# A two-layer decoder trunk with routed experts: one-hot rows written a chunk ahead, small experts two chunks behind the large ones

## The chip, the cores and the metric

The kernel runs on one core of one Trainium2 chip, in one launch. The time is the device time of the program in microseconds (us), smaller is better. Engines are named as in the profile: PE is TensorE (PEld its weight load), DVE VectorE, ACT ScalarE, POOL GpSimd, and SP the engine whose queue issues the DMAs here. The span runs from the first to the last instruction.

## The reference

A sequence of 256 tokens of width 1024 in float32 goes through two layers. Layer 0 has an attention and a state-space half and then a dense SwiGLU block; layer 1 has two kinds of attention and then a routed block of eight SwiGLU experts. The change lies in that last block alone:

```
logits = t @ router                       # t: 256 tokens x 1024, after an RMS norm
top_val, top_idx = top_k(logits, 2)       # two of eight experts for each token
top_w = softmax(top_val)
gates = sum(one_hot(top_idx, 8) * top_w)
for e in range(8):                        # each expert has 1024 -> 2816 -> 1024
    out += gates[:, e] * ((silu(t @ w_gate[e]) * (t @ w_up[e])) @ w_down[e])
return x + out
```

The weights of one expert are 3 x 1024 x 2816 floats. All eight experts are read from memory once, which is 264 pieces ("units") of 1 MB.

## The kernel before, in words

Up to the routing, a recorder (lines 71 to 317) takes down the operations and writes them out in an order of its own. From the first expert on the recorder is off (line 1629), and every engine gets its instructions in the order in which the code is written.

The eight experts are sorted by how many tokens chose them. The first four (BIG = 4) are "large": they get 128 rows each, and each product is made of three matmuls on split operands (a high part wh and a low part wl, lines 522 to 524). The last four are "small": 64 rows each, in plain float32, two of them side by side on PE.

An expert is worked in 11 chunks (FC) of 256 hidden columns. A chunk has three units of weights: gu0 and gu1 (gate and up columns, for the two halves of the input width) and dn (the down rows). The list `steps` (lines 1594 to 1605) sets the order: chunk g of the large experts runs beside chunk g - LAG of the small ones, LAG being 4. So the first LAG chunks belong to large experts alone, and the last ones to small experts alone.

Before an expert can start, its rows must be picked from the 256 normalised tokens (xnh and xnl are their high and low part). That is a matmul with a one-hot matrix: `one_hots` writes the matrix on DVE by comparing positions (poso) with a row of counters, and `gather_all` makes one of the eight 128-row products and lets ACT write it out. Both are called in the step "rest", which follows gu1 of a large chunk (lines 1672 to 1689): the small experts' products (into xs) in the first chunks of the first large expert (p = 0), those of large experts 1 and 2 (into xl) from chunk LAG + 2 of p = 0 on, and those of large expert 3 from chunk 2 of p = 1 on.

```
def one_hots(lo, n, width=P):
    t = tw(2 * n * width, dt=F32R).rearrange("p (b e s) -> p b e s", b=2, e=n)
    for b in range(2):
        V.tensor_tensor(t[:, b], ..., ..., OP.is_equal)     # DVE
def gather_all(k, oh, dst):
    o, gain = gather(k, ..., n * w)                         # four matmuls on PE
    S.activation(dst[:, :, k], ..., AF.Copy, scale=gain)    # ACT
```

Ahead of "rest", the step gu1 does the elementwise part of the chunk and calls `st.ahead(HL)` twice (lines 1653 to 1655): each call splits one coming unit of a large expert into wh (two ACT instructions) and wl (two DVE instructions), until three units stand ready. A third call follows after the transposes ("tr"). The tile `tw` is one of a set of 12 working tiles.

The units come in the order in which the steps use them, through the class `Stream`. It has twelve places to load into: five tiles "raw", and xres, xg0, xg1 (both "xg" in the profile), more, fl, wx and wy. xg0 is given up once 14 units have been asked for (XG = 14), because xl is put there. A large unit's place is free once it is split, a small unit's once PE has read it. Loads are issued on SP in one queue, in order. The units of the first large expert lie at a fixed address; all others need the expert's number from the routing (`ids`, read into a register by SP at line 1615). While the recorder is on, `load` stops at the first unit whose address needs that number (lines 718 and 719).

Of the kernel before, what the change touches and what calls it, by code (L numbers as in the profile page):

```python
# [19 lines left out]
P = 128  # L20
# [32 lines left out]
XG = 14  # L53
BIG = 4
HALFP = 64
LAG = 4
PAIRED = 0.65
WARM = 10
FIRST = 9
# [335 lines left out]
def kernel(ctx: ExitStack, tc: tile.TileContext, a, out: bass.AP):  # L395
# [29 lines left out]
    def tw(n=512, np_=P, dt=F32):  # L425
        return rec.tile(wkp, [P, 512], dt, "tw", TW, name="tw")[:np_, :n]

    def pa():
        return rec.tile(psp, [P, 512], F32, "ps", 8, name="ps")
# [104 lines left out]
    def bc(ap, shape):  # L534
        return ap.to_broadcast(shape)
# [237 lines left out]
    def ff_gu(st, xs, gu, u, ahead=True):  # L773
        wh, wl = st.next(ahead)
        for b in range(len(xs)):
            for kk in range(4):
                k = 4 * u + kk
                mm3(gu[b], xs[b][0][:, k, :], xs[b][1][:, k, :], wh[:, kk * 512:(kk + 1) * 512],
                    wl[:, kk * 512:(kk + 1) * 512], k == 0, k == 7)

    def ff_act(gu, scales=None, act=None):
        hs = []
        for b in range(len(gu)):
            si = tw(256)
            hh = tw(256)
            if scales:
                tact(si, gu[b][:, 0:256], AF.Silu, scale=scales[b])
                V.scalar_tensor_tensor(hh, gu[b][:, 256:512], scales[b], si, op0=OP.mult, op1=OP.mult)
            else:
                (act or tact)(si, gu[b][:, 0:256], AF.Silu)  # L790
                V.tensor_tensor(hh, gu[b][:, 256:512], si, OP.mult)
            hs.append(hh)
        return hs

    def ff_tr(hs):
        n = 2 * len(hs) * P
        tp = pa()
        transposes([h[:, i * P:(i + 1) * P] for i in range(2) for h in hs], tp)
        th, tl = tw(n, dt=F32R), tw(n, dt=F32R)
        S.activation(th, tp[:, :n], AF.Copy)  # L800
        V.tensor_tensor(tl, tp[:, :n], th.bitcast(F32), OP.subtract)
        return th, tl
# [73 lines left out]
    for g in range(2):  # L876
# [13 lines left out]
        for c in range(4):  # L890
            j = 4 * g + c
# [188 lines left out]
    mo = scope("m")  # L1080
# [389 lines left out]
# [4 lines that stand above are left out]
            V.tensor_tensor(t[:, b], bc(iota[:, None, 0:width], [P, n, width]),  # L1474
                            bc(poso[:, b, lo:lo + n, None], [P, n, width]), OP.is_equal)
        return t

    def both_halves(r):

        t = tw(256, dt=F32R).rearrange("p (b s) -> p b s", b=2)  # L1480
        for b in range(2):
            V.tensor_scalar(t[:, b].rearrange("p (i s) -> p i s", i=2), bc(iota[:, None, 0:HALFP], [P, 2, HALFP]),
                            poso[:, b, r:r + 1], None, op0=OP.is_equal)
        return t
# [6 lines left out]
    def gather(k, ohs, n):  # L1491

        o = pa()[:, 0:n]
        for i, src in enumerate((xnh, xnl)):
            for b in range(2):
                mmx(o, src[:, b, k * P:(k + 1) * P], ohs(b), i + b == 0, i + b == 2)
        return o, k2("gf1k", k, k + 1)
# [5 lines left out]
    def gather_all(k, oh, dst):  # L1503

        n, w = oh.shape[2], oh.shape[3]
        o, gain = gather(k, lambda b: oh[:, b].rearrange("p e s -> p (e s)"), n * w)
        S.activation(dst[:, :, k], o.rearrange("p (e s) -> p e s", e=n), AF.Copy, scale=gain)
# [17 lines left out]
    def scatter(t, y, g, acc, store=False):  # L1525
        for i in range(2):
            rec.late = HALF if i else 0
            cs = slice(i * 512, (i + 1) * 512)
            for b in range(2):
                sp = pa()  # L1530
                T.matmul(sp, t[:, b * P:(b + 1) * P], y[i][0], start=True, stop=False)
                T.matmul(sp, t[:, b * P:(b + 1) * P], y[i][1], start=False, stop=True)
                V.scalar_tensor_tensor(acc[:, b, cs], sp, g(b), acc[:, b, cs], op0=OP.mult, op1=OP.add)
                if store:
                    dma(ov[:, b, cs], acc[:, b, cs])
        rec.late = 0
# [5 lines left out]
    def large_split(src):  # L1542
        x = large_tile()
        S.activation(x[0], src, AF.Copy)
        V.tensor_tensor(x[1], src, x[0].bitcast(F32), OP.subtract)
        return x


    def sm_gu(xs, gu, u):
        w = st.next(False)  # L1550
        for kk in range(4):
            k = 4 * u + kk
            wv = w[:, kk * 512:(kk + 1) * 512].rearrange("p (g f) -> p g f", g=2)
            for i in range(2):
                mmx(gu[i * HALFP:(i + 1) * HALFP, 0:256].rearrange("p (g f) -> p g f", g=2), xs[:, k],
                    wv[:, :, i * P:(i + 1) * P], k == 0, k == 7)
        st.done()

    def sm_act(gu):
        si, hh = tw(P), tw(P)  # L1560
        tact(si, gu[:, 0:P], AF.Silu)
        V.tensor_tensor(hh, gu[:, P:256], si, OP.mult)
        return hh

    def sm_tr(hh):
        tp = pa()
        transposes([hh], tp)
        t = tw(P)
        S.activation(t, tp[:, 0:P], AF.Copy)
        return t  # L1570

    def sm_dn(t, y, first, last):
        w = st.next(False)
        for hf in range(2):
            for i in range(2):
                mmx(y[hf][i * HALFP:(i + 1) * HALFP, :], t[:, i * HALFP:(i + 1) * HALFP],
                    w[:, i * 1024 + hf * 512:i * 1024 + (hf + 1) * 512], first, last)
        st.done()
# [12 lines left out]
    def chunk(sm, g):  # L1591
        return (sm, *divmod(g, FC)) if 0 <= g < BIG * FC else None

    steps = []
    for g in range(BIG * FC + LAG + 1):
        l, l0, s, s0 = chunk(False, g), chunk(False, g - 1), chunk(True, g - LAG), chunk(True, g - LAG - 1)
        if l and s0:
# [38 lines left out]
    for n, (k, it) in enumerate(steps):  # L1636
        if k == "late":
            while pend:
                scatter(*pend.pop(0))
            continue  # L1640
        sm, p, c = it
        if k in ("gu0", "gu1"):
            if k == "gu0":
                gu[sm] = pa()
            if sm:
                sm_gu(xs[:, p], gu[sm], unit_of[k])
            else:
                ff_gu(st, [xb], [gu[sm]], unit_of[k], False)
            if k == "gu1":
                hs[sm] = sm_act(gu[sm]) if sm else ff_act([gu[sm]])  # L1650
                if not sm and c == FC - 1 and p < BIG - 1:
                    xb = large_split(xl[:, p % 2])
                if not sm:
                    st.ahead(HL)
                    st.ahead(HL)
                if c == 0:
                    ohs[sm] = n, both_halves(BIG + p) if sm else one_hots(p, 1)[:, :, 0]
        elif k == "tr":
            ts[sm] = sm_tr(hs[sm]) if sm else ff_tr(hs[sm])
            if not sm:  # L1660
                st.ahead(HL)
        elif k == "dn":
            if c == 0:
                ys[sm] = [pa(), pa()]
            if sm:
                sm_dn(ts[sm], ys[sm], c == 0, c == FC - 1)
            else:
                ff_dn(st, ts[sm], [ys[sm]], c == 0, c == FC - 1, False)
            if c == FC - 1:
                r = p + (BIG if sm else 0)  # L1670
                pend.append((ohts[sm], y_split(ys[sm]), lambda b, r=r: gateo[:, b, r:r + 1], x3, n == len(steps) - 2))
        else:
            for e in list(ohs):
                if n >= ohs[e][0] + 5:
                    o = ohs.pop(e)[1]
                    ohts[e] = oht_of(o[:, 0], o[:, 1])
            if p == 0 and c < LAG:
                for j in range(2 * c, 2 * c + 2):
                    gather_all(j, oh_s, xs)
            if p == 0 and LAG + 2 <= c < LAG + 6:  # L1680
                if c == LAG + 2:
                    xl, oh_l = mo([P, 2, 8, P], "xg0"), one_hots(1, 2)
                for j in range(2 * (c - LAG - 2), 2 * (c - LAG - 1)):
                    gather_all(j, oh_l, xl)
            if p == 1 and 2 <= c < 6:
                if c == 2:
                    oh_l = one_hots(3, 1)
                for j in range(2 * c - 4, 2 * c - 2):
                    gather_all(j, oh_l, xl[:, 0:1])
    man.close()  # L1690
# [179 lines left out]
```

## Time and profile before

| | us |
|---|---|
| median of 3 runs (1150.53 to 1153.55) | 1151.38 |
| the profiled execution | 1152.82 |
| its span | 1151.0 |
| PE busy | 1113.1 (97%) |
| DVE busy | 723.1 (63%) |
| ACT busy | 601.4 (52%) |
| DMA queue, share of 16 engines' span | 76.0% |

The expert stage starts near 469 us and takes the rest of the span. A PE that is shown as busy is not at its peak, as matmuls overlap: what counts is where the next one starts. Two other things are to be read beside it, the granted clock (1.00 is 2.4 GHz, 0.50 is 1.2 GHz) and the rate at which the DMA queue moves bytes. The first queue that runs without a gap is a limit of its own, whatever PE does.

### The profile page before, as it was taken

The numbers are of one execution on the slowest core, as the hardware profiler recorded it, in microseconds if no ns is written. First come the engines' busy times: TensorE is split into PE (matmuls) and PEld (weight loads), VectorE is DVE, ScalarE is ACT, GpSimd is POOL, SyncE is SP. The second block draws the span as 40 slices with busy tenths as digits, with TensorE's granted clock in tenths as the row PEclk, the third lists the DMA queues.
The fourth block names the chain that finished last, engine by engine and source line by source line (L and its number), as shares of the span: only waits on it lengthen the run. The fifth ranks groups of instructions, "written<-read, shape, count | busy, mean of one in ns | idle before, by whom it ended". The sixth has DMA issues, their size and how long they took to land.

```text
span 1151.0 us, 16659 instructions
## 1 busy us (share of the span) xinstructions
PE 1113.1 (97%) x6100; PEld 833.5 (72%) x6100; DVE 723.1 (63%) x1325; ACT 601.4 (52%) x1134; POOL 29.1 (3%) x59
## 2 busy tenths in 40 slices
PE   8999999999999999998999799999999999999997
PEld 7887888888787877875676567666666666676653
DVE  6999954544388867785356646556556556565542
ACT  5868644444378656474355435545454554544430
POOL 1050000000300000000000000000000000000000
PEclk9999999999999999899899999999999999999999
DMA  9551555556343633379799989999999999999996
GB/s 345 214 215 37 185 218 188 186 181 218 113 156 124 254 149 147 144 272 382 289 401 408 411 333 390 414 422 422 421 421 420 423 421 422 421 422 422 421 422 248
DMA packets 52216, 348.15 MB, mean 302 GB/s; under 512 B 5920, under 2 KB 6048, under 8 KB 11680
## 3 DMA queue, kind: packets, MB, share of 16 engines
q1 hardware_dynamic: 52128, 347.02, 76.0%
q8 instruction: 50, 0.82, 0.3%
q14 instruction: 38, 0.31, 0.1%
HBM read 345.95 MB, written 1.05 MB: 301 GB/s over the span
## 4 chain that ended last, share of the span: by engine, by line
PE 89%; DMA 5%; DVE 3%; ACT 2%; issue 0%; SPq 0%; DVEq 0%; ACTq 0%
PE ps L333 23%; PE ps L522 19%; PE ps L524 19%; PE ps L523 19%; PE ps L328 10%; DMA raw<-in_moe_dram 3%; DMA more<-in_moe_dram 2%; DVE wl L333 1%; ACT tw L328 1%; DMA raw<-in_w_dram 0%; DVE wl L328 0%; DVE tw L328 0%; ACT wh L333 0%; DVE xres L333 0%; ACT wh L328 0%
## 5 line engine op out<-in xcount | busy, mean ns | idle before, releaser
L333 ACT ACTIVATE tw<-ps 128x256 fp32r<-128x256 f32 (+3 forms) x202 | 72.6, 365 | 360.8 <-PE ps L524 212.5
L522 PE MATMUL ps<-wh,fh 128*128 128x512 f32 (+2 forms) x632 | 254.5, 403 | 0.0
L523 PE MATMUL ps<-wl,fh 128*128 128x512 f32 (+2 forms) x632 | 245.5, 389 | 0.0
L333 DVE TENSOR_TENSOR tw<-ps,tw 128x256 f32<-128x256 f32 (+3 forms) x158 | 64.6, 427 | 264.7 <-ACT tw L333 264.7
L333 DVE TENSOR_TENSOR wl<-raw,wh 128x1024 fp32r<-128x1024 f32 x156 | 183.7, 1224 | 55.9 <-ACT wh L333 55.4
L333 ACT ACTIVATE wh<-raw 128x1024 fp32r<-128x1024 f32 x156 | 155.2, 1050 | 43.7 <-PE ps L524 37.8
L524 PE MATMUL ps<-wh,fh 128*128 128x512 f32 x352 | 138.5, 394 | 0.0
L522 PEld LDWEIGHTS ps<-wh,fh 128*128 128x128 f32 x632 | 119.4, 189 | 22.2 <-issue 0.2
L523 PEld LDWEIGHTS ps<-wl,fh 128*128 128x128 f32 x632 | 119.4, 189 | 21.7 <-issue 0.2
L524 PE MATMUL ps<-wh,fl 128*128 128x512 f32 (+2 forms) x280 | 107.6, 384 | 0.0
L522 PE MATMUL ps<-wh,tw 128*128 128x512 f32 (+1 forms) x252 | 103.2, 410 | 1.8 <-ACT tw L333 1.1
L524 PE MATMUL ps<-wh,tw 128*128 128x512 f32 (+1 forms) x252 | 99.3, 394 | 0.0
L523 PE MATMUL ps<-wl,tw 128*128 128x512 f32 (+1 forms) x252 | 99.2, 394 | 0.0
L333 PE MATMUL ps<-raw,xs 128*64 128x256 f32 x672 | 78.4, 379 | 0.0
L524 PEld LDWEIGHTS ps<-wh,fh 128*128 128x128 f32 x352 | 66.4, 189 | 14.5
L328 DVE TENSOR_TENSOR wl<-raw,wh 128x512 fp32r<-128x512 f32 x113 | 74.7, 680 | 2.9 <-ACT wh L328 2.9
L333 PEld LDWEIGHTS ps<-raw,xs 128*64 128x64 f32 x672 | 47.9, 137 | 33.4 <-issue 11.7
L328 ACT ACTIVATE wh<-raw 128x512 fp32r<-128x512 f32 (+1 forms) x104 | 59.7, 620 | 18.7 <-PE ps L524 11.5
L524 PEld LDWEIGHTS ps<-wh,fl 128*128 128x128 f32 x280 | 52.6, 188 | 10.7 <-DVE fl L328 0.2
L522 PEld LDWEIGHTS ps<-wh,tw 128*128 128x128 f32 x252 | 47.6, 189 | 15.0 <-ACT tw L333 2.2
L524 PEld LDWEIGHTS ps<-wh,tw 128*128 128x128 f32 x252 | 47.4, 188 | 11.4 <-DVE tw L328 0.4
L523 PEld LDWEIGHTS ps<-wl,tw 128*128 128x128 f32 x252 | 47.5, 189 | 9.3
(319 smaller groups left out, 1744.2 us busy)
## 6 DMA issues: line engine op xcount, KB each, us to landing
raw<-in_moe_dram SPq DMA_DIRECT2D x120, 1024.0 KB, 13.9
raw<-in_ffn_dram SPq DMA_DIRECT2D x30, 1024.0 KB, 4.8
xg<-in_moe_dram SPq DMA_DIRECT2D x24, 1024.0 KB, 13.4
more<-in_moe_dram SPq DMA_DIRECT2D x24, 1024.0 KB, 12.9
fl<-in_moe_dram SPq DMA_DIRECT2D x24, 1024.0 KB, 13.2
raw<-in_w_dram SPq DMA_DIRECT2D x23, 1024.0 KB, 4.9
wx<-in_moe_dram SPq DMA_DIRECT2D x23, 1024.0 KB, 14.2
xres<-in_moe_dram SPq DMA_DIRECT2D x23, 1024.0 KB, 14.0
```

Of the source, the lines that this page charges most:

```text
L328: return (self.name, self.cost(fn, args, kw), lambda: real(*args, **kw))
L333: return getattr(self.eng, fn)(*args, **kw)
L522: nc.tensor.matmul(ps, xh, wh, start=start, stop=False)
L523: nc.tensor.matmul(ps, xh, wl, start=False, stop=False)
L524: nc.tensor.matmul(ps, xl, wh, start=False, stop=stop)
```

## The change

Three things are done. LAG goes from 4 to 2: the small experts run two chunks behind the large ones. The eight products for the small experts are made four a chunk in two chunks, not two a chunk in four. And the one-hot matrices of large experts 1 and 2, and of large expert 3, are written in the "rest" of the chunk before the one whose "rest" has their first product (chunk 3 of p = 0, with products from chunk 4 on; chunk 1 of p = 1, with products from chunk 2 on). Products for large experts 1 and 2 also start two chunks earlier, since they are placed by LAG.

```
-LAG = 4
+LAG = 2
...
             if p == 0 and c < LAG:
-                for j in range(2 * c, 2 * c + 2):
+                for j in range(8 // LAG * c, 8 // LAG * (c + 1)):
                     gather_all(j, oh_s, xs)
+            if (p, c) in ((0, LAG + 1), (1, 1)):
+                oh_l = one_hots(1, 2) if p == 0 else one_hots(3, 1)
             if p == 0 and LAG + 2 <= c < LAG + 6:
                 if c == LAG + 2:
-                    xl, oh_l = mo([P, 2, 8, P], "xg0"), one_hots(1, 2)
+                    xl = mo([P, 2, 8, P], "xg0")
                 for j in range(2 * (c - LAG - 2), 2 * (c - LAG - 1)):
                     gather_all(j, oh_l, xl)
             if p == 1 and 2 <= c < 6:
-                if c == 2:
-                    oh_l = one_hots(3, 1)
                 for j in range(2 * c - 4, 2 * c - 2):
                     gather_all(j, oh_l, xl[:, 0:1])
```

How instructions move is shown at three places. The first is DVE, in the first large expert, where the one-hot matrix of large experts 1 and 2 is written (`tw<-c_2935,poso 128x256`; `wl<-..` rows are splits, `tw<-ps,tw` the elementwise part of a chunk, CAST the copy of a transposed one-hot). Before:

```order
L333 CAST tw<-ps 128x256
L333 TENSOR_TENSOR tw<-ps,tw 128x128
L333 TENSOR_TENSOR tw<-ps,tw 128x256
L333 TENSOR_TENSOR wl<-wy,wh 128x1024 x2
L333 TENSOR_TENSOR tw<-ps,tw 128x256
L333 TENSOR_TENSOR wl<-raw,wh 128x1024 x4
L333 TENSOR_TENSOR tw<-c_2935,poso 128x256 x2
L333 TENSOR_TENSOR tw<-ps,tw 128x128
```

And with the change:

```order
L333 TENSOR_TENSOR tw<-ps,tw 128x256
L333 TENSOR_TENSOR wl<-raw,wh 128x1024 x2
L333 TENSOR_TENSOR wl<-xres,wh 128x1024 x2
L333 CAST tw<-ps 128x256
L333 TENSOR_TENSOR tw<-c_2935,poso 128x256 x2
L333 TENSOR_TENSOR tw<-ps,tw 128x128
L333 TENSOR_TENSOR tw<-ps,tw 128x256
L333 TENSOR_TENSOR wl<-raw,wh 128x1024 x2
L333 TENSOR_TENSOR tw<-ps,tw 128x256
L333 TENSOR_TENSOR wl<-xg_5203,wh 128x1024 x2
```

The two rows stand behind four rows of splits in both, but with the change the products that read them come one chunk later on PE.

The second place is SP's queue at the end of the recorded part: the loads up to the one that reads the expert's number (L1615), the difference of the two.

```order
 L447 DMA xg_3415<-in_moe_dram 128x2048
 L447 DMA raw<-in_moe_dram 128x2048 x4
-L447 DMA wx<-in_moe_dram 128x2048
 L447 DMA xres<-in_moe_dram 128x2048
-L447 DMA wy<-in_moe_dram 128x2048
-L447 DMA raw<-in_moe_dram 128x2048
-L447 DMA xg_3422<-in_moe_dram 128x2048
-L447 DMA more<-in_moe_dram 128x2048
-L447 DMA fl<-in_moe_dram 128x2048
 L447 DMA raw<-in_moe_dram 128x2048
 L1615 TENSOR_LOAD ids
```

With the one raw load ahead of this piece, 14 units are loaded before the number is known in the kernel before, and 8 with the change, because the ninth unit is now one of a small expert. Behind L1615 the changed queue goes on:

```order
L1615 ISA x2
L443 ISA
L443 DMA raw<-in_moe_dram 128x2048
L443 ISA
L443 DMA xg_4964<-in_moe_dram 128x2048
L443 DMA more<-in_moe_dram 128x2048
L443 DMA fl<-in_moe_dram 128x2048
L443 DMA wx<-in_moe_dram 128x2048
L443 ISA
L443 DMA wy<-in_moe_dram 128x2048
L443 ISA
L443 DMA raw<-in_moe_dram 128x2048
```

Six of the moved loads stand here, as the first of the loads with a run-time address.

The third place is ACT at the first chunks, where the small experts' products are written out (xs); the difference of the two.

```order
 L333 ACTIVATE wh<-raw 128x1024 x4
-L333 ACTIVATE xs<-ps,c_2935 128x4x64 x2
+L333 ACTIVATE xs<-ps,c_2935 128x4x64 x4
 L333 ACTIVATE tw<-ps 128x256
 L333 ACTIVATE wh<-xres 128x1024 x2
 L333 ACTIVATE tw<-ps 128x256
 L333 ACTIVATE wh<-xg_3415 128x1024 x2
```

The first chunk has two more of these instructions behind its four split rows, and the second chunk likewise; the third and fourth have none. PE has 4090 rows in both kernels.

## Rows read from the trace of the kernel before

**Rows 1.** The page: PE's line, and the issue line of the expert loads.

```profile
PE 1113.1 (97%) x6100; PEld 833.5 (72%) x6100; DVE 723.1 (63%) x1325; ACT 601.4 (52%) x1134; POOL 29.1 (3%) x59
raw<-in_moe_dram SPq DMA_DIRECT2D x120, 1024.0 KB, 13.9
```

**Rows 2.** Two long windows: length, engines' busy time, granted clock, DMA share, GB/s.

```profile
467.70:725.00 257.30, 244.05 (x1319) 177.76 (x1319) 149.78 (x193) 127.78 (x193) 0.00 (x0) 0.96 0.88 347
725.00:1136.00 411.00, 407.69 (x2313) 277.27 (x2313) 235.75 (x286) 195.08 (x284) 0.00 (x0) 1.00 1.01 420
```

**Rows 3.** Whom PE waited for from 460 us on: total, times, longest.

```profile
PE ps L333 <- DVE tw L333: 15.6, 6, 6.5
```

**Rows 4.** The timeline around 541 us: start, length, engine, idle before.

```profile
542.50 4.63 DVE L333 TENSOR_TENSOR wl<-raw,wh 128x1024 fp32r<-128x1024 f32 x4 [0.52 <-ACT wh L333]
...
547.05 0.75 DVE L333 TENSOR_TENSOR tw<-c,poso 128x256 fp32r<-128x256 f32 x2
...
547.62 0.82 PE L333 MATMUL ps<-tw,xnh 128*128 128x256 f32 x2 [6.51 <-DVE tw L333]
...
548.90 0.47 ACT L333 ACTIVATE xg<-ps,c 128x256 f32<-128x256 f32 x1 [3.60 <-PE ps L333]
```

**Rows 5.** The timeline at 662 us.

```profile
662.40 0.66 PE L333 MATMUL ps<-tw,xnh 128*128 128x128 f32 x2 [6.37 <-DVE tw L333]
```

**Rows 6.** A short window of PE behind the first wait: length, PE, clock, DMA share, GB/s.

```profile
547.60:550.00 2.40, 2.38 (x10) 0.50 0.93 341
```

**Rows 7.** The chain of waits in order of time: start, length, engine, tile, line.

```profile
526.79 5.91 PE ps L333 x44
...
565.89 6.63 PE ps L333 x50
580.94 6.63 PE ps L333 x50
...
641.71 5.91 PE ps L333 x44
...
679.51 6.53 PE ps L333 x50
694.44 6.53 PE ps L333 x50
...
813.41 5.91 PE ps L333 x44
827.72 5.69 PE ps L333 x42
841.82 5.69 PE ps L333 x42
```

**Rows 8.** PE's timeline of the first chunk ends (a product, chunk 1, chunk 1's product).

```profile
476.04 0.40 PE L333 MATMUL ps<-tw,xnh 128*128 128x256 f32 x2
...
476.99 0.40 PE L522 MATMUL ps<-wh,fh 128*128 128x512 f32 x1
...
485.68 0.48 PE L333 MATMUL ps<-tw,xnh 128*128 128x256 f32 x2
```

**Rows 9.** Windows of 15 us, columns as in rows 2.

```profile
470.00:485.00 15.00, 15.00 (x67) 12.28 (x67) 9.98 (x21) 8.76 (x13) 0.00 (x0) 0.94 0.38 148
...
560.00:575.00 15.00, 15.00 (x89) 10.75 (x87) 8.08 (x10) 7.73 (x12) 0.00 (x0) 1.00 0.65 253
```

**Rows 10.** SP's queue: the first loads with a run-time address.

```profile
467.67 14.93 SPq L443 DMA_DIRECT2D raw<-in_moe_dram  x3
```

**Rows 11.** The end of the chain of waits.

```profile
1089.34 19.81 DMA more<-in_moe_dram
...
1116.07 22.81 PE ps L333 x156
...
1139.23 1.99 PE ps L333 x8
```

**Rows 12.** The last window with loads in it, columns as in rows 2.

```profile
1138.00:1140.00 2.00, 1.63 (x9) 0.48 (x7) 0.00 (x0) 0.28 (x1) 0.00 (x0) 1.00 0.23 88
```

## The prediction, made before the changed kernel was run

> **What bounds the kernel now.** The page comes first: PE is busy for 97% of the span, and every expert load is 1024 KB [rows 1]. That share hides stages with different limits, so the windows of the expert stage come next. Until 725 us the DMA queue is short of work (347 GB/s), from there on it runs at 420 GB/s with a busy share of 1.01 [rows 2]. So two things could set the end: PE, which does the same work whenever it comes, and a queue that is full in the last 411 us but has idle time in the first 257. The list of waits says what PE stands still for: DVE, six times, 15.6 us in all, 6.5 at the longest [rows 3]. The timeline shows the two large ones. At 547.62 PE starts the first product for large experts 1 and 2 after 6.51 us idle; on DVE the one-hot matrix was written at 547.05, straight behind four splits of 4.63 us [rows 4]. At 662.40 the same happens for large expert 3, 6.37 us [rows 5]. Behind such a wait the granted clock is 0.50, that is 1.2 GHz [rows 6]. At the very end the chain runs through a load, 19.81 us from 1089 on, and then 22.81 us of small experts' products on PE [rows 11].
>
> **The one-hots, part by part.** What a wait costs is read from the pace of the chunks, which takes the slow clock in. The chain has one row a chunk [rows 7]. A chunk after a x44 row takes 827.72 - 813.41 = 14.31 us, a plain one 841.82 - 827.72 = 14.10, one with two products of large experts 1 and 2 takes 580.94 - 565.89 = 15.05, one with two of expert 3 takes 694.44 - 679.51 = 14.93. Without the first wait, 526.79 + 14.31 + 15.05 would bring PE to 556.15; the row stands at 565.89. That is 9.74 us: 6.51 idle and 3.2 of slow clock. Without the second, 641.71 + 14.31 + 14.93 = 670.95, and the row stands at 679.51: 8.56 us, of which 6.37 is idle. Together 18.3 us.
>
> The change writes both matrices one chunk earlier, over 14 us before their first reader. The two DVE instructions still cost 0.75 us and 0.48 or so, but in a window like 560 to 575 DVE is busy for 8.08 of 15 us [rows 9], and nothing on PE asks for them in that chunk. If that cover were gone, the price would be these 0.75 us. What is late next at these places is nothing that the trace shows: the tokens' parts xnh and xnl have lain ready since the first products. I take the whole 18.3 us as gone.
>
> **Four products a chunk.** PE makes two products in 476.99 - 476.04 = 0.95 us [rows 8]; eight products cost 3.8 us in two chunks as in four. On ACT a product's output takes 0.47 us [rows 4]. Two more of them in each of the first two chunks, 0.94 us, stand ahead of the copy of the transposes that the down product needs, while ACT is busy for 8.76 of 15 us there [rows 9]. Bounds: nothing, if that copy is still ready when PE has made the products and gu1, and 0.94 us twice if it is late by all of it. PE itself comes 0.95 us later at this point because it makes the two products too, so I take nothing.
>
> **LAG 2 on PE.** PE has as many instructions as before. Two chunks of small experts' work move from the end, where small experts run alone, to the front. At full clock they cost the same there, so the sum is nothing.
>
> **LAG 2 on the DMA queue.** This is the part with a cost that can go either way. A unit is 1.0486 MB, which at 420 GB/s [rows 2] is 2.50 us. Before, 250 units are loaded from 467.67 on [rows 10], now 256, since the ninth unit is already a small expert's and waits for the expert's number. If the queue never pauses, the 256 units take 639 us and the last lands at 1107. Before, 250 units take 624 us, but the last ends near 1138.4 (in the window from 1138 the queue moves 88 GB/s for two us, 0.4 us of work [rows 12]): 46.4 us were gaps, nearly all ahead of 725 (467.7 to 725 at 347 instead of 420 GB/s is 45 us of them).
>
> How many gaps remain? There are 12 places and 3 split units. At 467.67 eight units have been asked for and three are split, so seven places are free, and the queue has 7 x 2.50 = 17.5 us of work at once, where before one free place was followed by a stop: its first three loads went out over 14.93 us [rows 10]. By then PE has moved on. Chunk 0 ends at 476.04, four products take 1.90, chunk 1 takes 485.68 - 476.99 = 8.69 [rows 8], again 1.90 and 8.69: at 497.2 PE has used eight units, and the queue can have brought 8 + 29.5 / 2.50 = 19.8, against room for 14 + 8 = 22. The room is not reached, though places come free in lumps after splits; I allow 4 us of gaps, with 0 and 10 as ends. From then on a pair of chunks uses six units in 14.10 to 15.05 us and the queue brings 5.6 to 6.0, so places stay free. The last load then lands at about 1111.
>
> PE's last down product ended at 1139.23 + 1.99 = 1141.2 [rows 11]; 18.3 us less is 1122.9. The queue is ahead of that by 12 us where it was ahead by 2.8 before. Six small units instead of twelve follow the last unit that must be split, which asks for a lead a little larger; 12 us leaves room. So PE decides and the gain stays. Of the waits behind late loads at the end, which are the 15.6 - 6.51 - 6.37 = 2.7 us left in rows 3, all may go, or 3 more may come, as the queue's lead is drawn down by plain chunks just as before; I take 1 us less.
>
> **The sum.** 18.3 + 1.0 = 19.3 us. The profiled execution took 1152.82 us for a span of 1151.0, so one like it would take 1133.5; the median of the runs is 1.44 below that execution, which gives 1132.1. With the ends named above (2.7 less, or 3 more and 1.9 for the outputs) the gain lies between 13.4 and 21.0 us, 1130 to 1138.
>
> **Rivals.**
>
> *The queue takes part of it back.* Gaps stay because SP issues in order: one load whose place is not free holds up all behind it, as in the 14.93 us of rows 10. If half of the old gaps stay, 23 us, the last load lands at 1130; with the 2.8 us from there to PE's end, some 2 for the shorter tail, and 9.8 from PE's end to the span's, the span is 1144.6, the time 1145. For it: the queue is full for all of the last 411 us [rows 2]. Against: seven places are free at once, and the early chunks use units faster than before. From 13 us of gaps on it costs something, from 31 on nothing is left of the gain.
>
> A page bears on this: the Trainium skill, "DMA: Bandwidth & Descriptors", section "Where 436 GB/s comes from", says that loads from HBM are bound by the HBM side at some 358 GB/s for a core. By that rule 256 units would take 750 us and no change of PE's order could gain. This trace does not bear it out: 420 GB/s over 411 us in rows 2, so the measurement decides, and that rule gets no chance of its own.
>
> *The missing early loads decide.* This is the case on the other side. Six loads that used to land before the expert's number was known come after it, 15 us of queue time. If the gaps behind 467.67 all stay (46.4 us), the last load lands at 1153, and by the same steps the time is 1168. It decides once more than 31 us of gaps stay. For it: 250 and 256 units at the measured rate. Against: the gaps came from full places, and 467.67 is now a time at which seven are empty.
>
> *A wait comes back elsewhere.* xl is written two chunks earlier and lies in the place xg0, and with four products at once more PSUM tiles and more of the twelve working tiles are held. If one such thing stops PE for as long as one of the old waits did, 9 us are lost again: 1142. Nothing in the rows speaks for it except that two waits of this kind did arise.
>
> *It does nothing that can be measured.* Under 0.3% (3.5 us, about what a measurement here can tell from no change), if the queue keeps some 30 us of gaps.
>
> **How the numbers follow.** The forecast 0.70 (0.08 of it below 1130, by waits at the end or a better front than counted), the queue taking part back 0.13, a wait elsewhere 0.09, nothing 0.04, the missing early loads 0.04. The range of eight in ten is 1125 to 1142: it leaves out most of the queue's case and the last two. Faster 0.92, within 0.3% 0.04, slower 0.04.
>
> **What would show it.** In the new profile no idle of 6 us before a product on PE, and a granted clock of 1.00 from about 480 us on; the one-hot rows on DVE one chunk ahead of the first product; the first seven loads behind 467 us within 2 us on SP's queue; the rate above 400 GB/s from 470 us on instead of 347; the row after the first products one chunk's pace behind the one before. The prediction is wrong if PE waits more than 5 us for loads in the last 100 us, if the queue stands still between 485 and 600 us for more than 13 us in all, or if a new wait of some us stands at the first chunks.

## The result, and the profile after

| | before | with the change |
|---|---|---|
| median of 4 runs each | 1152.05 (1150.53 to 1153.55) | 1136.47 (1135.60 to 1137.66) |
| ratio, 95% interval | | 0.9865 (0.9850 to 0.9879) |
| the profiled execution and its span | 1152.82, 1151.0 | 1137.01, 1135.2 |

The change saves 15.6 us (13.9 to 17.3 by the interval). The forecast was 19.3: the sign and the cause are right, some 3.7 us of it did not arrive.

The page of the changed kernel, PE's line, beside [rows 1]:

```profile
PE 1108.8 (98%) x6100; PEld 830.9 (73%) x6100; DVE 723.4 (64%) x1325; ACT 601.3 (53%) x1134; POOL 29.1 (3%) x59
```

PE, with the same 6100 instructions, is busy for 4.3 us less. That is about the slow clock that is gone behind the two waits (3.2 and 8.56 - 6.37 = 2.2 us) less the 1.3 us of it that came at the end (below). The list of waits from 460 us on has this in place of [rows 3] (total, times, longest):

```profile
PE ps L333 <- DVE tw L333: 4.3, 5, 2.7
```

The two long waits are gone from it. The two long windows answer to [rows 2], with the same columns (length, engines' busy time, granted clock, DMA share, GB/s):

```profile
467.70:725.00 257.30, 256.93 (x1447) 185.06 (x1447) 154.99 (x200) 133.31 (x204) 0.00 (x0) 0.99 0.99 406
725.00:1121.00 396.00, 390.89 (x2186) 267.31 (x2184) 227.42 (x275) 189.22 (x274) 0.00 (x0) 1.00 1.00 416
```

In the first, PE no longer stands still (256.93 of 257.30 us, 244.05 before), and the queue moves 406 instead of 347 GB/s. In the second PE is idle for 5.1 of 396 us, before for 3.3 of 411. So the loss must be sought there.

The chain of waits gives the place. Its rows of 44 matmuls stand at the same chunk of large experts 1 to 3 in both kernels (start, length, engine, tile, line). With the change:

```profile
642.61 5.91 PE ps L333 x44
...
805.76 5.91 PE ps L333 x44
...
965.98 5.91 PE ps L333 x44
...
1111.94 11.35 PE ps L333 x74
1123.70 1.99 PE ps L333 x8
```

Before, beside 641.71 and 813.41 in [rows 7] and 1139.23 in [rows 11], the third one:

```profile
973.20 5.91 PE ps L333 x44
```

With the change PE has done two chunks of a small expert more at each of the first three rows. What those are worth is seen at the end: 22.81 us of matmuls before [rows 11] against 11.35 now, 11.46 us. So the changed kernel is ahead by 641.71 + 11.46 - 642.61 = 10.6 us after the first one-hots, by 813.41 + 11.46 - 805.76 = 19.1 after both, by 973.20 + 11.46 - 965.98 = 18.7 at the third row, and by 1139.23 - 1123.70 = 15.5 at the last product. Of each figure 0.44 us were there already at the first product for the small experts (475.60 against 476.04 in [rows 8]). So what was forecast for the one-hots, 18.3 us, had arrived (18.2 at the third row); 3.2 us of it are lost again after 966.

The timeline of PE there (start, length, engine, operation, idle before and who ended it):

```profile
1100.70 1.90 PE L333 MATMUL ps<-wx,xs 128*64 128x256 f32 x16
...
1102.89 1.95 PE L333 MATMUL ps<-more,xs 128*64 128x256 f32 x16
1107.51 0.48 PE L333 MATMUL ps<-cp,tw 128*128 128x128 f32 x1 [2.67 <-DVE tw L333]
...
1108.21 0.63 PE L523 MATMUL ps<-wl,tw 128*128 128x512 f32 x1
1108.64 0.63 PE L524 MATMUL ps<-wh,tw 128*128 128x512 f32 x1
...
1111.87 1.94 PE L333 MATMUL ps<-wy,tw 128*64 128x512 f32 x8
```

And ACT and DVE in the same stretch:

```profile
1103.80 2.00 ACT L333 ACTIVATE wh<-raw 128x1024 fp32r<-128x1024 f32 x2 [6.11 <-DMA raw<-in_moe_dram]
1105.71 0.53 ACT L333 ACTIVATE tw<-ps 128x128 f32<-128x128 f32 x2
...
1104.89 2.36 DVE L333 TENSOR_TENSOR wl<-raw,wh 128x1024 fp32r<-128x1024 f32 x2 [6.74 <-ACT wh L333]
1107.17 0.62 DVE L333 TENSOR_TENSOR tw<-ps,tw 128x128 f32<-128x128 f32 x2
```

Read it backwards. PE stands at the transposes of a small chunk (1107.51) and waits for that chunk's elementwise product on DVE (1107.17). The product's inputs were ready near 1102.6, when PE had finished this chunk's gate and up products (1100.70 + 1.90); the row at 1102.89 belongs to the next small chunk. But ACT and DVE work in order, and ahead of it stands the split of the last unit of the last large expert, and that unit landed only at 1103.80. A late load thus stops work that does not need it. The Trainium skill has the rule, "PSUM — Partial Sum Buffer", section "Engine vs sequencer instructions": the queues of ScalarE and VectorE are strictly first in, first out. The trace agrees, with the product at 1107.17 behind the split at 1104.89. Behind the wait the matmuls start 0.43 us apart, not 0.23, and the window of PE says why (columns as above):

```profile
1107.50:1110.30 2.80, 2.79 (x7) 2.26 (x8) 0.28 (x1) 0.28 (x1) 0.00 (x0) 0.50 1.00 389
```

The granted clock is 0.50, 1.2 GHz, for 2.8 us.

### The profile page after: what moved, and what is told of

The parts are those of the page before. It is cut to its first block, busy times and chain, and to the rows that moved or that the text cites. A ratio compares the mean times of both kernels' runs of the same rounds, so it can differ in the third digit from the quotient of the medians.

```text
span 1135.2 us, 16665 instructions
## 1 busy us (share of the span) xinstructions
PE 1108.8 (98%) x6100; PEld 830.9 (73%) x6100; DVE 723.4 (64%) x1325; ACT 601.3 (53%) x1134; POOL 29.1 (3%) x59
## 4 chain that ended last, share of the span: by engine, by line
PE 82%; DMA 12%; DVE 3%; ACT 2%; issue 1%; SPq 0%; DVEq 0%; ACTq 0%
PE ps L333 19%; PE ps L522 18%; PE ps L524 18%; PE ps L523 18%; PE ps L328 10%; DMA raw<-in_moe_dram 4%; DMA wx<-in_moe_dram 3%; DMA wy<-in_moe_dram 2%; DMA fl<-in_moe_dram 2%; DVE wl L333 1%; DMA xg<-in_moe_dram 1%; ACT tw L328 1%; DMA raw<-in_xT_dram 0%; ACT wh L333 0%; DVE wl L328 0%
## 5 line engine op out<-in xcount | busy, mean ns | idle before, releaser
L333 DVE TENSOR_TENSOR wl<-raw,wh 128x1024 fp32r<-128x1024 f32 x166 | 195.7, 1223 | 66.1 <-ACT wh L333 65.4
L333 DVE TENSOR_TENSOR tw<-ps,tw 128x128 f32<-128x128 f32 (+3 forms) x158 | 64.4, 427 | 246.9 <-ACT tw L333 246.9
L333 ACT ACTIVATE wh<-raw 128x1024 fp32r<-128x1024 f32 x166 | 165.3, 1050 | 50.9 <-PE ps L524 37.8
L333 PE MATMUL ps<-raw,xs 128*64 128x256 f32 x624 | 72.9, 379 | 0.0
L328 ACT ACTIVATE wh<-raw 128x512 fp32r<-128x512 f32 (+1 forms) x103 | 59.2, 620 | 18.7 <-PE ps L524 11.5
L333 PEld LDWEIGHTS ps<-raw,xs 128*64 128x64 f32 x624 | 44.6, 137 | 30.8 <-issue 10.4
## 6 DMA issues: line engine op xcount, KB each, us to landing
fl<-in_moe_dram SPq DMA_DIRECT2D x23, 1024.0 KB, 13.9
```

The costliest lines, as they stand in the source:

```text
L328: return (self.name, self.cost(fn, args, kw), lambda: real(*args, **kw))
L333: return getattr(self.eng, fn)(*args, **kw)
```

## The experiments

Each was timed in five rounds beside the kernel before, four to eleven runs of each; a ratio is to that kernel, with its 95% interval. The runs that are compared in one paragraph did not all share a chip, so ratios are compared, not times, and a difference of under some 1.5 us between two variants is not told apart by times. Where the text says so, traces are compared instead.

**The one-hots without LAG 2.**

```
-LAG = 2
+LAG = 4
```

> The changed kernel with LAG back at 4 (and so two products a chunk in four chunks); only the one-hot matrices are written a chunk earlier. My theory: the two waits of PE are worth 18.3 us, the order of large and small experts is worth nothing ahead of the last 130 us, and LAG 2 gives some 3 us back at the end, where the last unit that must be split comes only six units ahead of the end of the queue. Then this kernel stands at 1152.0 - 18.3 = 1133.7 us, some 2.8 us faster than the changed kernel, with about 2.7 us of waits of PE behind late loads as in the kernel before. Rival 1, the loss at the end comes from PE being early against a full queue whatever LAG is: 1136.5 us, as the changed kernel. Rival 2, LAG 2 brings something of its own at the front: slower than 1137.

Measured: 1132.97 us (1132.42 to 1134.60), ratio 0.9836 (0.9823 to 0.9849). That is 19.0 us off, 3.5 more than the whole change. Its chain of waits:

```profile
526.51 5.91 PE ps L333 x44
...
631.70 5.91 PE ps L333 x44
...
794.85 5.91 PE ps L333 x44
...
1098.14 22.80 PE ps L333 x156
1121.29 1.99 PE ps L333 x8
```

These rows do the same work as those of [rows 7] and [rows 11], so they can be subtracted directly. It comes to the first row, ahead of any one-hot of large experts, 0.28 us earlier. Without that it is ahead by 641.71 - 631.70 - 0.28 = 9.73 us after the first wait, by 813.41 - 794.85 - 0.28 = 18.28 after the second. The prediction had 9.74 and 18.30. At the end it is 1139.23 - 1121.29 - 0.28 = 17.7: it gives back 0.6 where the change gives back 3.2. So the one-hots carry the whole gain, and the loss at the end came in with LAG 2.

**The first one-hots alone**, LAG 4, those of large expert 3 left where they were:

```
+            if (p, c) == (0, LAG + 1):
+                oh_l = one_hots(1, 2)
...
                 if c == 2:
                     oh_l = one_hots(3, 1)
```

> The kernel before (LAG 4, two products a chunk) with only the first pair of one-hots, those of large experts 1 and 2, written a chunk earlier; those of large expert 3 stay where they were. My theory: the two waits are priced separately, this one at 9.74 us, so 1152.0 - 9.7 = 1142.3 us, and the 6.4 us wait for large expert 3 stays. Rival: the first wait is in part hidden, since while PE stands the queue fills up places that later chunks draw on, so that less than 7 us come through: 1145 us or more.

Measured: 1142.52 us (1141.28 to 1145.79), ratio 0.9923 (0.9908 to 0.9938), which is 8.9 us off (7.1 to 10.6). One of the two waits stays:

```profile
650.97 0.66 PE L333 MATMUL ps<-tw,xnh 128*128 128x128 f32 x2 [6.38 <-DVE tw L333]
```

The chain:

```profile
525.10 5.91 PE ps L333 x44
...
630.28 5.91 PE ps L333 x44
```

(526.79 - 525.10 = 1.69 us earlier at the first row, 641.71 - 630.28 = 11.43 at the second: 9.74 from the wait.) The two waits are priced separately, as the prediction had them. The rival, that the queue makes use of PE's standing still, falls.

**LAG 2 and four products without the one-hots**, each matrix written in the step of its first product again:

```
-            if (p, c) in ((0, LAG + 1), (1, 1)):
-                oh_l = one_hots(1, 2) if p == 0 else one_hots(3, 1)
...
+                    xl, oh_l = mo([P, 2, 8, P], "xg0"), one_hots(1, 2)
...
+                if c == 2:
+                    oh_l = one_hots(3, 1)
```

> The changed kernel with the one-hot matrices written where they were, in the chunk of their first product; so LAG 2 and four products a chunk alone. Both waits of PE (6.5 and 6.4 us idle) should be there again. My theory: PE is then some 18 us later, the queue stays as early as in the changed kernel (last load near 1118 to 1125 us), so no late loads at the end: 1152.0 less the 2.7 us of old waits, 1149 to 1151. Rival, the short tail of LAG 2 costs its 3 us in any case: 1155. Rival, LAG 2 pays by itself and the one-hots do little: below 1145.

Measured: 1152.77 us (1149.76 to 1155.69), ratio 1.0009 (0.9996 to 1.0022): nothing that can be told, and my expectation of a small gain was wrong. It had PE some 18 us later and the queue as early as with the change. PE is later, but so is the queue: up to 725 us it moves 377 GB/s and not 406, and its last load lands near 1136.4 and not 1118.2.

```profile
467.70:725.00 257.30, 244.06 (x1331) 174.29 (x1332) 143.40 (x187) 123.97 (x188) 0.00 (x0) 0.95 0.93 377
...
1136.00:1138.00 2.00, 2.00 (x19) 1.36 (x20) 0.00 (x0) 0.28 (x1) 0.00 (x0) 1.00 0.24 85
```

That is 7.9 us ahead of the end of PE's last product (1142.28 + 1.99), where with the change it is 7.5: the loads have hardly more lead, so this run does not show what more lead would do. PE's timeline has the wait at the end, and its chain of waits what it costs:

```profile
1125.89 0.47 PE L333 MATMUL ps<-cp,tw 128*128 128x128 f32 x1 [2.43 <-DVE tw L333]
...
1127.02 0.63 PE L524 MATMUL ps<-wh,tw 128*128 128x512 f32 x1
1127.44 0.63 PE L522 MATMUL ps<-wh,tw 128*128 128x512 f32 x1
```

```profile
984.33 5.91 PE ps L333 x44
...
1142.28 1.99 PE ps L333 x8
```

Counted as for the change, this kernel is ahead of the one before by 973.20 + 11.46 - 984.33 = 0.3 us at the third row and behind by 1142.28 - 1139.23 = 3.05 at the last product. So 3.4 us go at the end, as with the change (3.2), though no one-hot has moved: the loss comes with LAG 2. Six small units stand there behind the last one that must be split, twelve with LAG 4. How much of it the times show stays open in part: the profiled execution (1155.6 us) is among the slowest of its eleven, and the runs say 1.0 us in all (-0.5 to 2.5).

**Lag 3 in between**, with the products made three, three and two a chunk:

```
-LAG = 2
+LAG = 3
...
-                for j in range(8 // LAG * c, 8 // LAG * (c + 1)):
+                for j in range(3 * c, min(8, 3 * (c + 1))):
```

> The changed kernel with LAG 3 (products for the small experts three, three and two a chunk). My theory: between the changed kernel and the one with LAG 4, 1134 to 1136 us, the waits at the end between 2.7 and 5.8 us. Rival 1 (the loss does not hang on LAG): 1136.5. Rival 2 (LAG 2 pays at the front): 1138.

Measured: 1134.79 us (1133.90 to 1136.52), ratio 0.9849 (0.9834 to 0.9864), between the two as expected, though the interval touches both. Its wait at the end is not shorter, but the clock behind it stays:

```profile
1102.50 0.33 PE L333 MATMUL ps<-cp,tw 128*128 128x128 f32 x1 [2.96 <-DVE tw L333]
...
1102.90 0.40 PE L523 MATMUL ps<-wl,tw 128*128 128x512 f32 x1
1103.14 0.39 PE L524 MATMUL ps<-wh,tw 128*128 128x512 f32 x1
```

By the rows of its chain (961.01 at the third row, 1105.63 with 17.22 us for the small experts at the end, 1123.20 at the last product) it is ahead by 973.20 + 22.81 - 17.22 - 961.01 = 17.8 us and then by 1139.23 - 1123.20 = 16.0. It gives back 1.8 us, between the 0.6 of LAG 4 and the 3.2 of LAG 2.

**The six early loads.** The kernel before, kept from asking for more than eight units before the expert's number is known:

```
-                if rec.on and callable(self.srcs[j]):
+                if rec.on and (j >= 8 or callable(self.srcs[j])):
```

> The kernel before with one limit more: while the recorder is on, only eight units are asked for, not fourteen (the other six follow as soon as it is off). LAG and the one-hots are as before. My theory: the six late loads go into places that are free and into time in which the queue stood still anyway, so the time stays at 1152 within 1.5 us. Rival, the six loads are 15 us of queue time that the full queue lacks at the end: 1160 to 1167.

Measured: 1152.42 us (1150.80 to 1155.16), ratio 1.0004 (0.9993 to 1.0015). Its window behind 467.70:

```profile
467.70:725.00 257.30, 244.05 (x1314) 177.46 (x1314) 148.80 (x189) 127.03 (x191) 0.00 (x0) 0.96 0.89 355
```

The queue makes up for them in time in which it had stood still (355 against 347 GB/s in [rows 2]). The rival that had the missing early loads decide is out.

**The slow clock behind the last wait.** The changed kernel with 11 matmuls that nobody reads, in the 2.67 us:

```
+            if sm and (p, c) == (BIG - 1, FC - LAG - 1):
+                idle = pa()
+                for i in range(11):
+                    T.matmul(idle, ones[:, 0:P], ones, start=True, stop=True)
```

> The changed kernel with 11 more matmuls on PE, whose results nobody reads, put ahead of the transposes of the last step that large and small experts share. They fill the 2.67 us in which PE stands idle there and take nothing else away. My theory: the loss at the end is two things, the idle time (about 1.6 us more than in the kernel before) and the slow clock behind it (six matmuls 0.43 us apart where they were 0.23 apart, about 1.2 us). With PE kept at work the clock stays at 1.00 and only the second part goes: 1136.5 - 1.2 = 1135.3 us, and no matmul behind the wait at 0.43 us. Rival: the slow clock there is hidden behind the next load, so nothing is gained, 1136.5 us or, if the 11 matmuls reach beyond the wait, up to 1137.5.

Measured: 1135.12 us (1134.17 to 1136.02), ratio 0.9849 (0.9836 to 0.9862). PE's timeline:

```profile
1102.57 1.95 PE L333 MATMUL ps<-more,xs 128*64 128x256 f32 x16
1104.45 2.55 PE L333 MATMUL ps<-ones 128*128 128x512 bf16 x10
1107.06 0.33 PE L333 MATMUL ps<-cp,tw 128*128 128x128 f32 x1
...
1110.12 1.94 PE L333 MATMUL ps<-wy,tw 128*64 128x512 f32 x8
```

(The trace has ten records of the eleven matmuls.) From the next small chunk's first products (the rows x16) to the down product of the small chunk that waited (the rows x8) PE takes 1110.12 - 1102.57 = 7.55 us, in the changed kernel 1111.87 - 1102.89 = 8.98. Of the 1.43 us between them 0.13 lies ahead of the transposes (1107.06 - 1102.57 against 1107.51 - 1102.89), so 1.3 is the slow clock (1.2 was expected).

**The last large unit one place earlier in the queue:**

```
-            o = [("gu0", l), ("tr", l0), ("gu0", s if not l else None), ("tr", s0), ("gu1", l), ("dn", l0),
-                 ("late" if l else "", None), ("rest", l), ("dn", s0), ("gu0", s if l else None), ("gu1", s)]
+            o = [("gu0", l), ("tr", l0), ("tr", s0), ("gu1", l), ("dn", l0),
+                 ("late" if l else "", None), ("rest", l), ("dn", s0), ("gu0", s), ("gu1", s)]
```

> The changed kernel with one unit of weights moved in the last shared step: the last down unit of the large experts is loaded and used before the gate/up unit of the small expert that stood ahead of it. My theory: the 2.67 us wait on PE comes from this unit, the last that must be split; it landed at about 1103.8 us, and the small experts' elementwise work stands behind its split on ACT and DVE. One place earlier in the queue it lands some 2.5 us earlier, so the wait shrinks to some 0.2 us and with it goes the slow clock: 2.5 + 1.2 = 3.7 us at most, 1133 to 1134 us. Rival: the queue as a whole is late at the end, so that PE only waits for another load, with the same sum: 1136 to 1137 us.

Measured: 1134.76 us (1133.36 to 1136.65), ratio 0.9847 (0.9834 to 0.9861). The size was wrong:

```profile
1105.21 0.33 PE L333 MATMUL ps<-cp,tw 128*128 128x128 f32 x1 [2.10 <-DVE tw L333]
...
1123.33 1.94 PE L333 MATMUL ps<-fl,tw 128*64 128x512 f32 x8 [0.43 <-ACT tw L333]
```

The unit does land 2.3 us earlier (1101.50), but PE asks 1.8 us earlier too, since the small unit that it would have worked on now comes behind. 0.57 us of the wait go, the slow clock stays, and the last down product starts at 1123.33 against 1123.70. The ratios of the runs say 2.1 us, with intervals that overlap; the profiled execution is the slowest of its five (1136.65 us), and what the faster ones did is not shown. The same edit with LAG 4:

> Both one-hots a chunk early with LAG 4 (1132.97 us when run alone), and the last down unit of the large experts loaded one unit earlier. My theory: of the waits left at the end of that kernel (0.5, 0.6, 1.4 us) only the last hangs on this unit; it goes, without any slow clock to save: 1131.5 us, between 1131.3 and 1132.5. Rival: with eight units of small experts behind it the unit isn't what decides, and the time is the same, 1132.8 to 1133.2 us.

Measured: 1133.29 us (1132.48 to 1134.96), ratio 0.9835 (0.9822 to 0.9848), no difference to LAG 4 without it that the times can tell, and near the rival's number. In its trace the last wait is 0.86 us, without the edit 1.42.

**The split behind the small chunk's work.** If the wait is one of order on ACT and DVE, it must go when the order is turned round, with PE's instructions and the loads untouched:

```
-                if not sm:
+                if not sm and (p, c) != (BIG - 1, FC - 1):
                     st.ahead(HL)
                     st.ahead(HL)
```

(The call that follows the transposes then issues the split, behind the small chunk's elementwise part.)

> The changed kernel, in which only the last split of a large unit is issued later: on ACT and DVE it stands behind the elementwise work of the small chunk, no longer ahead of it; PE and the loads are as in the changed kernel. My theory: the wait of 2.67 us on PE is a matter of order on ACT and DVE. PE asks for the small chunk's product, whose inputs are ready at about 1102.6 us, but the product stands behind a split that waits for a load. With the order changed that wait goes; PE runs on to the large down product at about 1105.3 us and waits there for the first half of the split, until about 1106.2: some 0.9 us idle instead of 2.67, and perhaps no slow clock. Gain 1.8 to 3.5 us, 1133.0 to 1134.7 us if the changed kernel takes 1136.5. Rival: the load alone decides; PE then waits as long at the large down product, until 1107.5, and the time is the same, 1136 to 1137 us.

Measured: 1133.77 us (1133.28 to 1135.08), ratio 0.9841 (0.9827 to 0.9854). PE's timeline:

```profile
1102.02 1.95 PE L333 MATMUL ps<-more,xs 128*64 128x256 f32 x16
1103.89 0.33 PE L333 MATMUL ps<-cp,tw 128*128 128x128 f32 x1
1104.06 0.50 PE L522 MATMUL ps<-wh,tw 128*128 128x512 f32 x1
1105.32 0.50 PE L523 MATMUL ps<-wl,tw 128*128 128x512 f32 x1 [0.76 <-DVE wl L333]
...
1108.52 1.94 PE L333 MATMUL ps<-wy,tw 128*64 128x512 f32 x8
```

The 2.67 us are gone, 0.76 us come where the unit itself is needed, and the clock holds. The stretch takes 1108.52 - 1102.02 = 6.50 us where the changed kernel takes 8.98: 2.5 us back, within what was expected; by the medians' ratios 2.8. By its chain (965.11 at the third row, 1120.34 at the last product) it gives back 0.7 us of what the one-hots brought, where the change gives back 3.2. The rival (the load alone decides) falls: the unit landed late here too, at 1102.95 against 1103.80 in an execution that was 0.87 us behind this one at 966, and cost 0.9 us (0.76, and 0.17 at its second half). The same edit with LAG 4:

> Both one-hots a chunk early with LAG 4 (1132.97 us), and the last split of a large unit issued behind the elementwise work of the small chunk. My theory: the last wait there, 1.42 us, is of the same kind and mostly goes: 1132.97 - 1 = 1132 us, 1131.5 to 1132.7. Rival: with the longer tail this wait is hidden behind the queue, which then decides the end: 1132.8 to 1133.3 us.

Measured: 1134.34 us (1131.72 to 1135.12), ratio 0.9846 (0.9832 to 0.9859). The trace has 0.30 and 0.18 us of waits where there were 1.42, and a last product 2.89 us earlier, of which 1.74 were there before the one-hots (524.77 against 526.51 for the first row of the chain), so 1.2 us by the edit; the times don't show it. This kernel, LAG 4 with early one-hots alone, and LAG 2 with the split behind can't be told apart: 0.9836 to 0.9846. Each is faster than the change as made by 2 to 3.5 us in its median, with intervals that touch or nearly do.

## Why the prediction was right, and where it was not

*The one-hots: right to a tenth of a microsecond.* 9.74 and 18.30 us were forecast from the pace of the chunks; 9.73 and 18.28 were measured with LAG 4, 9.74 with the first one alone. Counting the idle time only would have given 12.9. On DVE the rows now stand a chunk ahead, at 515.52 us:

```profile
515.52 0.75 DVE L333 TENSOR_TENSOR tw<-c,poso 128x256 fp32r<-128x256 f32 x2
```

and the first product for large experts 1 and 2 follows at 523.38 us without a wait, beside 547.62 and 6.51 in [rows 4].

*Four products a chunk: nothing, as taken.* The first row of products in the chain and that of the third chunk stand at

```profile
475.76 1.91 PE ps L333 x16
...
496.86 3.97 PE ps L333 x34
```

and PE reaches the third chunk's products at 496.86 where 497.2 was worked out. The granted clock is 1.00 from 475 to 725 us.

*The missing early loads: nothing, as taken.* The run with eight early loads shows it for the kernel before, whose queue stood still for much of the time. With the change there is less room, and no run has LAG 2 with fourteen early loads. The nearest is LAG 4 with early one-hots, which has all fourteen: its last load lands near 1120.4, no earlier than the 1118.2 with the change. SP's first loads with a run-time address:

```profile
466.73 0.35 SPq L443 DMA_DIRECT2D raw<-in_moe_dram  x1
...
470.16 0.34 SPq L443 DMA_DIRECT2D raw<-in_moe_dram  x1
```

Seven of them go out in 3.4 us, not in 2, in place of three in 14.93 [rows 10].

*Gaps in the queue: 9 us instead of 4, at the edge of the bound of 10.* Two windows, beside [rows 9]:

```profile
485.00:500.00 15.00, 15.00 (x92) 11.80 (x92) 10.64 (x13) 9.11 (x13) 0.00 (x0) 1.00 0.79 310
500.00:515.00 15.00, 15.00 (x90) 10.28 (x86) 8.26 (x12) 7.18 (x11) 0.00 (x0) 1.00 0.87 347
```

Up to 725 us the queue moves 406 GB/s, and from there to 1107 some 421: 257.3 x (1 - 406 / 421) = 9.2 us of gaps, 6.6 of them in these two windows. SP issues no load between 485.07 and 495.09 us, which suggests that no place was free there, where the prediction had room left. The queue also loses some 3 us behind 1107, where the last three units, loaded in quarters, run at 257 to 360 GB/s. So the queue ends not at 1111 but near 1118:

```profile
1118.00:1120.00 2.00, 2.00 (x18) 1.09 (x16) 0.24 (x1) 0.28 (x1) 0.00 (x0) 1.00 0.13 46
```

The lead on PE's last product (1125.7) was 7.5 us, not 12.

*The term that failed: the waits behind late loads at the end.* "Of the waits behind late loads at the end [...] all may go, or 3 more may come, [...] I take 1 us less." 4.2 us of idle stand there (0.24, 0.55, 0.74, 2.67), 1.6 more than before, and 1.3 of slow clock behind the last: 2.9 us given back in place of 1 gained. That is 3.9 us against the forecast, about the 3.7 that are missing. The mechanism that decided was named in one sentence ("Six small units instead of twelve follow the last unit that must be split, which asks for a lead a little larger; 12 us leaves room") and its price was not worked out. The lead at the end of the queue was the wrong measure besides: the kernel with LAG 4 ends its queue near 1120.4 and PE's last product at 1123.3, 2.9 us apart and not 7.5, and gives less back. What counts is the time at which the last unit that must be split lands, and what stands behind that split on ACT and DVE. The gaps bear on it as well. The prediction had them cost something from 13 us on, by the end of the queue. Counted at the split, 2.67 us less of gaps would have taken the last wait away, so they cost something from some 6.5 us on (9.2 - 2.67); that is an estimate, and no run has the changed kernel with fewer gaps.

*The rivals.* The queue taking part back came nearest in kind, but not by gaps: half of the old 46 us was its condition, and 9 were left. A wait elsewhere came, not at the working tiles but at the split. It cost 2.9 us where 9 was its price.

## What to carry to other kernels

A wait's price is read from the pace of the stage with and without it, with the slow clock behind it; that was right to a tenth of a microsecond here. Where an engine works in order, an early-issued step that waits for a load holds up everything behind it, so near the end of a stream, where loads no longer lead, put work whose inputs are ready ahead of it. And a change that shortens the tail of a pipeline should be priced at the tail: which is the last load that needs preparing, when does it land, and what is queued behind it.

## What the runs showed of the hardware

The length of a wait did not by itself say whether the clock fell. Behind 2.10 us (the last unit earlier), 2.43 us (LAG 2 alone) and 2.67 us (the change) matmuls came 0.43 us apart for some 2.6 us, after 2.10 us only from 1.3 us behind the wait on; behind 2.96 us with lag 3 they kept 0.23 us apart, as they did behind 1.43 us in the kernel before:

```profile
1112.94 0.33 PE L333 MATMUL ps<-cp,tw 128*128 128x128 f32 x1 [1.43 <-DVE tw L333]
```

(The matmuls behind it start at 1113.34, 1113.58 and 1113.81.) What set these apart the runs don't show.

The queue of 1 MB loads moved 421 to 422 GB/s in each of the windows 725 to 900, 900 to 1000 and 1000 to 1100 us, in every kernel run here. While the last three units came in quarters of 256 KB it moved 257 to 395 in the windows from 1107 to 1118 us, with the change and with LAG 4. That the size of the loads is the reason is not shown, as no run loads these units whole.
